# Two-layer hybrid trunk on one core: TensorE in program order for the experts of layer 1, PSUM banks and weight slots re-dealt, and two of four row tiles normalised on TensorE

## The chip, the cores and the metric

The kernel runs on one core of one Trainium2 chip, as one launch. The metric is the device time of that launch in microseconds. Before the change three runs took 1233.72, 1237.96 and 1239.21 us; the median, 1237.96 us, is the time before.

A core has TensorE (PE in the profile; PEld is its weight load), VectorE (DVE), ScalarE (ACT), GpSimd (POOL) and SyncE (SP). SP computes nothing here: its queue issues most of the transfers, in the order in which they stand in it. ACT and POOL issue some transfers too.

## The reference, cut to what matters

A stream of 256 latent rows and 256 context rows, 1024 wide, goes through two layers. Each layer has a mixer (recurrences and attention in layer 0, two chunked state models in layer 1) and then a mixture of experts. Only the second half matters for the change:

```
h  = rms_norm(x, norm2_g) * (1 + m4) + m3          # m3 is the shift, a row of 1024 for the latents
hc = rms_norm(xc, norm2_g) * (1 + mc4) + mc3       # context rows, layer 0 only
out = 0
for e in range(16):                                # two of the 16 experts per row, by a gate
    hid = silu(t @ w1[e]) * (t @ w3[e])
    out = out + gate[:, e:e+1] * (hid @ w2[e])
x = x + m5 * out
```

Layer 0 sends 512 rows through its experts, layer 1 only the 256 latent rows. The weights of 16 experts are 96 MB in each layer, and each is used once.

## The kernel before, in words

**Memory.** One big SBUF tile, `arena_f`, is cut by a small allocator (`Arena`): `F.get` hands out columns, `F.free` takes them back, and the next owner waits on the chip for the last reader of the columns. What is left over becomes weight slots of 2048 columns (1 MB each). The class `Stream` keeps the list of all weight pieces in the order of their use, and issues the next piece on SP's queue whenever a slot is free (L159). `ws.add(F.fits(2048) - FA[l])` in `finish` (L1294) turns all whole free blocks but FA into slots; L1341 does the same with FB, and L1447 in `moe` with RES; `experts_rows` and `experts_sum` add what is left (L1612 and L1671). For layer 1, `swap` (L1355) also turns the split buffers `arena_rw` and `arena_rr` into six slots once the mixer is done with them. By the allocator's own count L1294 finds ten free blocks in layer 1 and makes eight of them slots, and the stage of the experts ends up with 19.

**Order.** The program is traced from Python, and a planner then orders the instructions of each engine by its own model of costs and due times. So an engine need not follow the order of the source. Each engine runs its list in that order, and waits at the head of the list. The planner also keeps two engines off one PSUM bank: a matmul into one half of a bank waits while another engine reads the other half.

**Layer 0, from the router to the first expert (`moe`, L1364).** `finish` leaves in `H` the rows x * (1 + m4) * norm2_g, unnormalised, two tiles of 128 latent rows (t = 0, 1) and two of context rows (t = 2, 3), and has laid down in DRAM, in `hd`, the shift row broadcast to all 512 rows (four transfers of 512 KB on ACT's queue, L1292). When the row norms `rs` are known, L1386 scales each tile on ACT (128x1024), and L1387 has POOL add it to `hd` by an accumulating transfer, 512 KB each. Meanwhile DVE computes the routing. The first expert's rows are gathered from `hd` by an indirect transfer of POOL (`gather`, L1474), transposed by TensorE (L1521, `take`) and multiplied (`first`, `hidden`, `second` in `experts_rows`), with every fp32 weight split in two by ACT (L322) and DVE or POOL (L325) and three matmuls for each product (L331 to L333).

**Layer 1, experts (`experts_sum`, L1656).** Weights are used unsplit. For each pair of experts `take` (L1700) selects up to 64 rows for each by 32 matmuls with a one-hot matrix. `first(e)` multiplies with w1 and then w3, 32 matmuls each (L1714), two weight pieces each, into the two halves of one PSUM bank; after w1 ACT takes a tanh (L1720) and DVE forms u (L1721), after w3 DVE finishes u (L1723). `hidden` transposes u (L1729) and ACT copies it out (L1730). `second` multiplies with w2, 16 matmuls (L1741) with two pieces; DVE applies the gate (L1746) and POOL adds the rows to the output by an indirect transfer (`scatter`, L1479). `rows` (L1681, L1683) are four small matmuls per expert that give row numbers and gates. The source interleaves them: w1(e), hidden(e-1), every other time take, rows(e+1), w3(e), second(e-1). The stream of pieces has the same order: w1 and w3 of e+1 before w2 of e.

PSUM has eight banks; `bank` deals them by tag, four to "a" (used by `first`, `second`), three to "b", one to "m".

**The shift row.** `mod_half` (L402) computes the modulation rows in eight steps of two layers by three groups by two halves; the rows of a half end in `ms`, biased by a DVE add (L425), and ACT's queue writes them to the DRAM tile `md` (L442). For l = 0, g = 1 the partitions 64 up hold m3.

## Time and profile before

| | |
|---|---|
| median of three runs | 1237.96 us |
| the profiled execution: its own time / its span | 1241.31 us / 1239.5 us |
| mean granted TensorE clock | 0.952 |
| busy: PE / DVE / ACT / POOL | 88% / 63% / 42% / 29% of the span |
| moved by transfers | 318.83 MB, 257 GB/s over the span |

The span runs from the first to the last instruction. All times in the rows are microseconds from the start of the span; durations of single groups are in ns where it says so. Busy shares are averages over stages with different limits, so the stages are read one by one: router of layer 0 at about 336 to 366 us, experts of layer 0 to about 670, mixer of layer 1 to about 990, experts of layer 1 from 1003 to the end. "PEclk" 1.00 is the clock of 2.4 GHz, 0.50 that of 1.2 GHz. A row of the timeline may stand for several instructions of one line (xN), from the start of the first to the end of the last; the ends of matmuls are modelled and overlap the next start, so pace is read from start to start.

### The profile page before, as it was taken

How to read it: one execution, taken by the hardware profiler on the slowest of the kernel's cores; microseconds unless marked ns; L12 is line 12 of the kernel's file. 1: busy time of each engine (PE TensorE's matmuls, PEld its weight loads, DVE VectorE, ACT ScalarE, POOL GpSimd, SP SyncE). 2: the span in 40 equal slices, each digit the busy share in tenths (PEclk: the TensorE clock that was granted, in tenths of full speed). 3: DMA queues.
4: the chain of work that ended last, by engine and by line, in shares of the span. 5: the costliest groups of instructions: out<-in, count | busy, mean ns of one | idle time of the engine just before them, and what ended most of it. 6: DMA issues, size and time to landing. Idle time of an engine off the chain costs nothing. (4 is left out here: it accounts for less than half of the span.)

```text
span 1239.5 us, 17204 instructions
## 1 busy us (share of the span) xinstructions
PE 1088.7 (88%) x6462; PEld 775.7 (63%) x6462; DVE 776.1 (63%) x1363; ACT 520.4 (42%) x799; POOL 360.9 (29%) x229
## 2 busy tenths in 40 slices
PE   3998979999829999999999788988997779999986
PEld 1666655656717777777777456655776766665552
DVE  2566737664639999999988754898477553222111
ACT  3355624443517787877887332333343210000000
POOL 1331513333213544545430321244242301111111
PEclk9998989999959999999999788999999889999998
DMA  9663468457277999999993135332387599999993
GB/s 354 215 221 123 167 178 279 157 192 282 109 214 259 347 356 352 366 352 357 352 356 119 73 140 139 132 139 90 122 301 267 226 374 409 413 421 419 409 412 96
DMA packets 76826, 318.83 MB, mean 257 GB/s; under 512 B 21290, under 2 KB 27530, under 8 KB 47936
## 3 DMA queue, kind: packets, MB, share of 16 engines
q1 hardware_dynamic: 54368, 293.58, 62.1%
q0 software_dynamic: 7200, 12.30, 4.7%
q10 hardware_dynamic: 15168, 11.76, 3.5%
q8 instruction: 54, 0.88, 0.3%
q14 instruction: 36, 0.29, 0.1%
HBM read 310.48 MB, written 18.96 MB: 266 GB/s over the span
## 5 line engine op out<-in xcount | busy, mean ns | idle before, releaser
L322 ACT CAST arena_rw<-arena_f 128x1024 fp32r<-128x1024 f32 x256 | 264.8, 1049 | 179.1 <-PE b L333 112.0
L325 DVE TENSOR_TENSOR arena_rw<-arena_f,arena_rw 128x1024 fp32r<-128x1024 f32 x198 | 259.3, 1348 | 84.9 <-ACT arena_rw L322 84.7
L331 PE MATMUL b<-arena_rw,arena_rr 128*128 128x512 f32 (+1 forms) x736 | 276.5, 376 | 3.0 <-ACT arena_rr L1217 1.1
L332 PE MATMUL b<-arena_rw,arena_rr 128*128 128x512 f32 (+1 forms) x736 | 274.1, 373 | 0.0
L333 PE MATMUL b<-arena_rw,arena_rr 128*128 128x512 f32 (+1 forms) x736 | 272.7, 372 | 0.0
L325 POOL TENSOR_TENSOR arena_rw<-arena_f,arena_rw 128x1024 fp32r<-128x1024 f32 x58 | 143.7, 2478 | 239.6 <-ACT arena_rw L322 220.8
L331 PEld LDWEIGHTS b<-arena_rw,arena_rr 128*128 128x128 f32 x736 | 140.4, 191 | 39.3 <-issue 9.8
L333 PEld LDWEIGHTS b<-arena_rw,arena_rr 128*128 128x128 f32 x736 | 139.8, 191 | 27.5 <-issue 4.1
L332 PEld LDWEIGHTS b<-arena_rw,arena_rr 128*128 128x128 f32 x736 | 140.6, 191 | 23.8 <-issue 1.3
L1479 POOL DMA_INDIRECT out<-arena_f x16 | 24.9, 1557 | 220.7 <-DVE arena_f L1746 216.8
L420 PE MATMUL b<-arena_f,cs 128*32 128x256 f32 x768 | 68.5, 412 | 22.3 <-DMA arena_f<-in_modw 22.1
L331 PE MATMUL b<-arena_rr,arena_rw 128*128 128x512 f32 (+1 forms) x192 | 75.3, 396 | 3.1 <-ACT arena_rw L322 1.4
L1714 PE MATMUL b<-arena_f 128*64 128x256 f32 x608 | 72.2, 381 | 4.5 <-DVE arena_f L1721 4.5
L333 PE MATMUL b<-arena_rr,arena_rw 128*128 128x512 f32 (+1 forms) x192 | 72.6, 381 | 3.9 <-DVE arena_rw L325 3.9
L1720 ACT ACTIVATE arena_f<-b 128x256 f32<-128x256 f32 x16 | 6.1, 384 | 165.9 <-PE b L1714 165.9
L332 PE MATMUL b<-arena_rr,arena_rw 128*128 128x512 f32 (+1 forms) x192 | 73.7, 385 | 0.8 <-POOL arena_rr L510 0.8
L1714 PEld LDWEIGHTS b<-arena_f 128*64 128x64 f32 x608 | 47.2, 137 | 26.8 <-DVE arena_f L1721 6.4
L420 PEld LDWEIGHTS b<-arena_f,cs 128*32 128x32 f32 x768 | 20.7, 112 | 55.3 <-issue 27.0
L1714 PE MATMUL b<-arena_f,arena_f 128*64 128x256 f32 x416 | 49.9, 381 | 1.9 <-DVE arena_f L1721 1.9
L331 PEld LDWEIGHTS b<-arena_rr,arena_rw 128*128 128x128 f32 x192 | 37.4, 196 | 18.7 <-issue 7.4
L1479 POOL DMA_INDIRECT yd<-arena_f x14 | 32.0, 2284 | 52.0 <-ACT arena_f L1569 52.0
L1474 POOL DMA_INDIRECT arena_f<-hd,arena_f x16 | 27.3, 1706 | 64.1 <-DVE arena_f L1514 50.5
(372 smaller groups left out, 1673.9 us busy)
## 6 DMA issues: line engine op xcount, KB each, us to landing
arena_f<-in_moe SPq DMA_DIRECT2D x192, 1024.0 KB
arena_f<-in_modw SPq DMA_DIRECT2D x96, 512.0 KB
arena_f<-in_wod SPq DMA_DIRECT2D x18, 1024.0 KB
arena_f<-in_wev SPq DMA_DIRECT2D x14, 1024.0 KB
arena_f<-md ACTq DMA_DIRECT2D x8, 512.0 KB
arena_f<-in_tok SPq DMA_DIRECT2D x4, 512.0 KB
yd<-arena_f SPq DMA_DIRECT2D x4, 512.0 KB
hd<-md ACTq DMA_DIRECT2D x4, 512.0 KB
```

The source lines that it names most:

```text
L322: nc.scalar.copy(h, raw)
L325: eng.tensor_tensor(l, raw, h.bitcast(F32), op=OP.subtract)
L331: nc.tensor.matmul(ps, ah, bh, start=first, stop=False)
L332: nc.tensor.matmul(ps, ah, bl, start=False, stop=False)
L333: nc.tensor.matmul(ps, al, bh, start=False, stop=last)
L420: nc.tensor.matmul(acc[32 * i:32 * i + 32, 0:256], self.cs[:, k, :], raw[:, i * 256:(i + 1) * 256], start=(k == 0), stop=(k == KC - 1))
L1474: self.nc.gpsimd.indirect_dma_start(out=xg, out_offset=None, in_=hd[:, :], in_offset=bass.IndirectOffsetOnAxis(ap=tk, axis=0), bounds_chec ...
L1479: self.nc.gpsimd.indirect_dma_start(out=yd[:, :], out_offset=bass.IndirectOffsetOnAxis(ap=dst, axis=0), in_=y, in_offset=None, bounds_chec ...
L1714: nc.tensor.matmul(p[64 * c:64 * c + 64, 256 * w:256 * w + 256], x[:, 4 * b + k], raw[:, 512 * k + 256 * c:512 * k + 256 * c + 256], start ...
L1720: nc.scalar.activation(u, p[:, 0:256], AF.Tanh, scale=0.5)
```

## The change

In layer 1, all TensorE instructions of the experts' loop are chained, each to the one traced before it, so that the planner must keep the order of the source (`in_order`). `first` takes one PSUM bank for w1 and another for w3. FA falls from 2 to 1 for both layers and RES from 3 to 2 for layer 0, so that one more block becomes a weight slot at those points.

In layer 0, the tiles of the latent rows no longer go through accumulating transfers. `mod_half` splits m3 into three bf16 terms (five small DVE operations and two more transfers on ACT's queue for each half) and stores them in `mb2`; `finish` loads them to three partitions, `S3`, and lays down the shift in DRAM for the context rows only. In `moe` ACT builds two diagonal matrices of `rs`; for each latent tile and each half of 512 columns TensorE multiplies the diagonal with `H` and adds ones times `S3` in the same bank, ACT copies the sum back over `H`, and SP's queue stores the tile to `hd` as a plain transfer. The context tiles are scaled and accumulated as before.

```diff
@@ -13,6 +13,8 @@
 AX = mybir.AxisListType
+PE = mybir.EngineType.PE
+NOSYNC = mybir.DependencyInfo(mybir.DependencyClass.NoSync, mybir.DependencyReason.DATA)
 
 P = 128
 D = 1024
@@ -235,8 +237,8 @@
 BQ = "sync"
 HR = 4
 HP = 0, 1, 0, 0
-RES = 3, 3
-FA = 2, 2
+RES = 2, 3
+FA = 1, 1
 FB = 9, 9
 NYY = 4
 WMK = 3
@@ -269,6 +271,22 @@
     def bank(self, tag="b"):
         self.n += 1
         return self.ps.tile([P, 512], F32, tag=tag, name=f"b{self.n}", bufs={"a": 4, "b": 3, "m": 1}[tag])
+
+    @contextmanager
+    def in_order(self, engine):
+
+        cur = self.nc.cur_bb
+        traced = cur.bb.instructions
+        last = traced[-1]
+        yield
+        traced = cur.bb.instructions
+        start = next(k for k in reversed(range(len(traced))) if traced[k] is last or traced[k].name == last.name) + 1
+        prev = None
+        for i in traced[start:]:
+            if i.engine == engine:
+                if prev is not None:
+                    self.tc.add_manual_dep(i, prev.name, NOSYNC, reason="in_order")
+                prev = i
 
     def dbg(self, name, ap):
         if self.dbgf is not None:
@@ -441,6 +459,16 @@
             for i in range(4):
                 nc.scalar.dma_start(self.md[l, g][:, h, i // 2, 256 * (i % 2):256 * (i % 2) + 256],
                                     ms[32 * i:32 * i + 2])
+            if (l, g) == (0, 1):
+
+                pt = F.get(3, 256, dt=BF)
+                for i in range(3):
+                    nc.vector.tensor_copy(pt[64:, i], ms[64:])
+                    if i < 2:
+                        nc.vector.tensor_tensor(ms[64:], ms[64:], pt[64:, i], op=OP.subtract)
+                for q in range(2):
+                    nc.scalar.dma_start(self.mb2[:, :, h, 256 * q:256 * q + 256], pt[64 + 32 * q:66 + 32 * q])
+                F.free(pt)
             F.free(ms)
         else:
             self.mr[l, h] = ms
@@ -1283,14 +1311,14 @@
 
         H = [F.get(2, D) for s in range(ns)]
         if ns == 2:
-
             self.hd = self.dp.tile([4 * P, D], F32, name=f"hd{l}")
-            for s in range(2):
-                src = self.md[l, 1][s, :, 1].rearrange("(o h) c -> o h c", o=1)
-                for i in range(2):
-                    t = 2 * s + i
-                    nc.scalar.dma_start(self.hd[t * P:(t + 1) * P, :].rearrange("p (h c) -> p h c", h=2),
-                                        src.to_broadcast([P, 2, 512]))
+
+            self.S3 = F.get(D, dt=BF)
+            nc.scalar.dma_start(self.S3[0:3], self.mb2[0].rearrange("i h c -> i (h c)"))
+            src = self.md[l, 1][1, :, 1].rearrange("(o h) c -> o h c", o=1)
+            for t in range(2, 4):
+                nc.scalar.dma_start(self.hd[t * P:(t + 1) * P, :].rearrange("p (h c) -> p h c", h=2),
+                                    src.to_broadcast([P, 2, 512]))
         self.ws.add(F.fits(2048) - FA[l])
 
         lg, hfR = [self.bank("m"), self.bank("a")][0:ns], Ring(F, 2, 2, 256)
@@ -1380,12 +1408,21 @@
             stt(L[:, t], lp[:, 32 * t:32 * t + 32], rs[:, t:t + 1], self.bR[:, t // 2], op0=OP.mult, op1=OP.add)
         if ns == 2:
 
-            H, hd = hd, self.hd
-            for t in range(nt):
-                h = H[t // 2][:, t % 2]
-                nc.scalar.activation(h, h, AF.Copy, scale=rs[:, t:t + 1])
-                nc.gpsimd.dma_start(hd[t * P:(t + 1) * P, :], h, accum_op=OP.add)
-            F.free(*H)
+
+            H, hd, dgR = hd, self.hd, F.get(2, P)
+            for t in range(2):
+                nc.scalar.activation(dgR[:, t], self.ident, AF.Copy, scale=rs[:, t:t + 1])
+            for t in range(2):
+                h, g = H[0][:, t], H[1][:, t]
+                nc.scalar.activation(g, g, AF.Copy, scale=rs[:, 2 + t:3 + t])
+                nc.gpsimd.dma_start(hd[(2 + t) * P:(3 + t) * P, :], g, accum_op=OP.add)
+                for c in range(2):
+                    sl, ps = slice(512 * c, 512 * c + 512), self.bank("a")
+                    nc.tensor.matmul(ps, dgR[:, t], h[:, sl], start=True, stop=False)
+                    nc.tensor.matmul(ps, self.oneb[0:3], self.S3[0:3, sl], start=False, stop=True)
+                    nc.scalar.copy(h[:, sl], ps)
+                nc.sync.dma_start(hd[t * P:(t + 1) * P, :], h)
+            F.free(*H, self.S3, dgR)
         tmp = []
 
         def T(n):
@@ -1705,22 +1742,24 @@
 
         def first(e):
             x = xs.pop(e)
-            p = self.bank("a")
+            ps = []
             for w in range(2):
+                p = self.bank("a")
                 for b in range(2):
                     raw = self.ws.take()
                     for k in range(4):
                         for c in range(2):
-                            nc.tensor.matmul(p[64 * c:64 * c + 64, 256 * w:256 * w + 256], x[:, 4 * b + k],
+                            nc.tensor.matmul(p[64 * c:64 * c + 64, 0:256], x[:, 4 * b + k],
                                              raw[:, 512 * k + 256 * c:512 * k + 256 * c + 256],
                                              start=(b == 0 and k == 0), stop=(b == 1 and k == 3))
                     self.ws.done(raw)
+                ps.append(p[:, 0:256])
                 if w == 0:
                     u = uR()
-                    nc.scalar.activation(u, p[:, 0:256], AF.Tanh, scale=0.5)
-                    nc.vector.scalar_tensor_tensor(u, u, 1.0, p[:, 0:256], op0=OP.add, op1=OP.mult)
+                    nc.scalar.activation(u, ps[0], AF.Tanh, scale=0.5)
+                    nc.vector.scalar_tensor_tensor(u, u, 1.0, ps[0], op0=OP.add, op1=OP.mult)
                 yield
-            nc.vector.scalar_tensor_tensor(u, u, 0.5, p[:, 256:512], op0=OP.mult, op1=OP.mult)
+            nc.vector.scalar_tensor_tensor(u, u, 0.5, ps[1], op0=OP.mult, op1=OP.mult)
             us[e] = u
 
         def hidden(e):
@@ -1746,20 +1785,21 @@
             nc.vector.scalar_tensor_tensor(y, py, gt, G2, op0=OP.mult, op1=OP.mult)
             self.scatter(half, y, dst)
 
...
+        with self.in_order(PE):
+            take(0)
+            rows(0)
+            for e in range(NE + 1):
+                f = first(e) if e < NE else iter(())
+                next(f, None)
+                if e:
+                    hidden(e - 1)
+                if e % 2 and e < NE - 1:
+                    take(e // 2 + 1)
+                if e + 1 < NE:
+                    rows(e + 1)
+                run_all(f)
+                if e:
+                    second(e - 1)
         F.free(ohR, phR, gtR, ddR, xR, uR, utR, yR, G2)
 
         def xt(xT, ohb, oh, cols):
@@ -1873,6 +1913,7 @@
         nc, tc, I, F, R = self.nc, self.tc, self.I, self.F, self.R
         w, m = self.sources(stages)
         self.ws, self.wm = Stream(nc, F, w, 2048), Stream(nc, F, m, 1024)
+        self.mb2 = self.dp.tile([2, 3, 2, 512], BF, name="mb2")
         self.md = {(l, g): self.dp.tile([2, 2, 2, 512], F32, name=f"md{l}{g}") for l in range(2) for g in (1, 2)}
         self.mr, self.sh, self.a2 = {}, [F.get(2, KC) for l in range(2)], [F.get(2, KC) for l in range(2)]
         self.rest = self.mods((1, 1), (1, 2)) if "l1" in stages else iter(())
```

## Rows read from the trace of the kernel before

**Rows 1.** Stretches: stretch, length, busy PE, PEld, DVE, ACT, POOL; PEclk, DMA share, GB/s.
```profile
500.00:525.00 25.00, 24.25 (x122) 19.48 (x121) 22.80 (x23) 20.16 (x25) 13.85 (x6) 1.00 1.00 369
...
985.00:990.00 5.00, 2.92 (x13) 2.11 (x14) 1.98 (x3) 1.92 (x5) 1.31 (x2) 0.52 0.01 2
...
1150.00:1200.00 50.00, 45.62 (x338) 25.61 (x336) 9.09 (x22) 2.27 (x6) 4.66 (x3) 1.00 1.02 413
```

**Rows 2.** Timeline of layer 0's router: start, length, engine, line [idle before it].
```profile
339.32 4.26 ACT L1386 ACTIVATE arena_f<-arena_f 128x1024 f32<-128x1024 f32 x4 [1.00 <-DVE arena_f L298]
...
340.79 2.90 POOL L1387 DMA_DIRECT2D hd<-arena_f  x3 [14.91 <-ACT arena_f L1386]
...
357.87 1.11 POOL L1474 DMA_INDIRECT arena_f<-hd,arena_f  x1 [13.13 <-DMA hd<-arena_f]
...
366.57 1.94 PE L1521 MATMUL b<-mskt,arena_f 128*128 128x128 f32 x8 [18.14 <-DMA arena_f<-hd,arena_f]
```

**Rows 3.** The stretch of the four accumulating transfers, columns as in rows 1.
```profile
342.00:356.00 14.00, 1.26 (x30) 1.03 (x30) 7.26 (x36) 1.82 (x4) 2.53 (x3) 0.50 0.88 152
```

**Rows 4.** Waits of SP's queue at 930 to 1000, 1003 to 1075, 1075 to 1200: total, times, longest.
```profile
SPq L159 <- PE b L333: 15.1, 1, 15.1
...
SPq L159 <- PE b L1714: 40.7, 17, 6.6
...
SPq L159 <- DMA arena_f<-in_moe: 104.7, 48, 3.5
```

**Rows 5.** Timeline of TensorE: the start of layer 1's experts.
```profile
1002.96 6.80 PE L1700 MATMUL b<-arena_f 128*128 128x128 f32 x32 [1.33 <-DVE arena_f L1452]
...
1009.77 1.95 PE L1714 MATMUL b<-arena_f,arena_f 128*64 128x256 f32 x16
```

**Rows 6.** Timeline of TensorE, 1020 to 1032 us: one of each step.
```profile
1020.93 0.44 PE L1729 MATMUL b<-mskt,arena_f 128*128 128x128 f32 x2
1021.20 3.74 PE L1700 MATMUL b<-arena_f 128*128 128x128 f32 x32
...
1024.95 3.67 PE L1714 MATMUL b<-arena_f 128*64 128x256 f32 x32
1028.45 3.60 PE L1741 MATMUL b<-arena_f 128*64 128x512 f32 x16
1031.89 0.39 PE L1714 MATMUL b<-arena_f 128*64 128x256 f32 x2
```

**Rows 7.** Timeline of TensorE: two experts in the second half of the stage.
```profile
1139.90 3.62 PE L1714 MATMUL b<-arena_f 128*64 128x256 f32 x32
1144.46 3.67 PE L1714 MATMUL b<-arena_f 128*64 128x256 f32 x32 [0.94 <-DVE arena_f L1721]
...
1169.89 3.62 PE L1714 MATMUL b<-arena_f,arena_f 128*64 128x256 f32 x32
```

**Rows 8.** Waits of TensorE, 1003 to 1230 us: total us, times, longest.
```profile
PE b L1714 <- DVE arena_f L1721: 6.3, 7, 0.9
PE b L1729 <- DVE arena_f L1723: 3.7, 7, 0.5
```

**Rows 9.** Stretches at the end of the weight stream, columns as in rows 1.
```profile
1218.00:1219.00 1.00, 1.00 (x12) 0.70 (x10) 0.00 (x0) 0.00 (x0) 0.00 (x0) 1.00 0.19 41
1219.00:1220.00 1.00, 1.00 (x14) 0.65 (x10) 0.00 (x0) 0.00 (x0) 0.00 (x0) 1.00 0.00 0
```

**Rows 10.** Timeline of all engines, 1221 us to the end.
```profile
1225.33 0.75 DVE L1746 SCALAR_TENSOR_TENSOR arena_f<-b,arena_f 128x512 f32<-128x512 f32 x1 [4.12 <-PE b L1741]
...
1226.36 1.55 POOL L1479 DMA_INDIRECT out<-arena_f  x1 [11.06 <-DVE arena_f L1746]
...
1228.77 0.75 DVE L1746 SCALAR_TENSOR_TENSOR arena_f<-b,arena_f 128x512 f32<-128x512 f32 x1 [2.68 <-PE b L1741]
1231.80 1.55 POOL L1479 DMA_INDIRECT out<-arena_f  x1 [3.88 <-DMA out<-arena_f]
```

**Rows 11.** Operations on L425, all times: duration in ns, minimum/median/maximum.
```profile
L425 DVE TENSOR_TENSOR arena_f<-b,arena_f x12: 405/424/425, 27.1 to 957.7; 128x256 f32<-128x256 f32 x12
```

More of the change, by code (lines that the diff above doesn't have):

```diff
@@ L1 @@
-from contextlib import ExitStack
+from contextlib import ExitStack, contextmanager
 import numpy as np
@@ L1747, in second @@
             self.scatter(half, y, dst)
-        take(0)
-        rows(0)
-        for e in range(NE + 1):
-            f = first(e) if e < NE else iter(())
-            next(f, None)
-            if e:
-                hidden(e - 1)
-            if e % 2 and e < NE - 1:
-                take(e // 2 + 1)
-            if e + 1 < NE:
-                rows(e + 1)
-            run_all(f)
-            if e:
-                second(e - 1)
+        with self.in_order(PE):
[13 more added lines that the diff above has]
+                    second(e - 1)
         F.free(ohR, phR, gtR, ddR, xR, uR, utR, yR, G2)
```

## The prediction

> **What bounds the kernel now.** I read the page's forty slices first, then a table of stretches, and then each stage that the change touches in its own timeline and waits. The experts of layer 0 are bound by the compute engines: in a stretch of 25 us TensorE is busy for 24.25 and VectorE for 22.8, and the weights are there in time [rows 1]. So what an earlier start saves there is kept, and a slot more in the middle of that stage is worth nothing. In front of it lies a hole: ScalarE scales four tiles in 4.26 us, GpSimd issues four accumulating transfers from 340.79 on, then waits 13.13 us for them, and gathers the first expert's rows at 357.87; TensorE sits idle 18.14 us until 366.57 [rows 2]. The routing is not what ends this wait; the transfers are.
>
> Layer 1's experts have two limits side by side. The transfers run full: DMA share 1.02 at 413 GB/s [rows 1]. Early on SP's queue waits for TensorE to release slots (40.7 us in 1003 to 1075), later only for its own earlier transfers (104.7 us in 1075 to 1200) [rows 4]. TensorE for its part never stands waiting for a weight: its waits are for DVE [rows 8]. Both hold because TensorE lags behind the stream: the last weights land by about 1218.9, when the share falls to zero [rows 9], but the last gate operation starts at 1228.77 [rows 10], though one half of `second`, under 2 us, is all that needs the last piece. What ends last there is TensorE.
>
> **Layer 1, TensorE's order and the banks.** From start to start, one step costs [rows 6]: hidden 0.27, take with rows 3.75, a w half 3.50, second 3.44. Two experts in the order of the source take four halves (14.0), two seconds (6.9), two hiddens (0.5), one take and two rows (3.9): 25.3 us, 12.7 for one. In the second half the planner put w1, w3 and hidden of one expert in a row. Then w3's matmuls wait 0.94 us for DVE's reading of the same bank, and hidden waits for DVE's last operation; two experts take 1169.89 - 1139.90 = 30.0 us [rows 7]. Over the stage these two waits are 6.3 and 3.7 us [rows 8]. Bound to the source, `second` of the expert before (3.44 us) lies between w3 and hidden, which covers the second wait; a bank of its own for w3 removes the first. Four "a" banks for three uses per expert give each bank back one expert after its reader is done, so I cost that at nothing; the cover is w1 of the next expert, and without it the price is the 0.9 of rows 8.
>
> From w1 of expert 0 at 1009.77 [rows 5] the whole list needs 32 halves (112.0), 16 seconds (55.0), 7 takes with rows (26.3), 16 hiddens and the other rows (6): 199 us, so TensorE could be done at 1209. It is then the weights that end last. The new chain makes the queue wait at its head for each piece, but the pieces come in the same order, so nothing is held that could run.
>
> **Layer 1, the slot.** The stream stands idle before the stage: DMA share 0.01 in 985 to 990 [rows 1], because SP's head waits 15.1 us for the mixer's last matmuls to release the six late slots [rows 4]. The new slot stands ahead of these in the list, and its columns held keys of the state model, freed before the merge; so 1 MB more lands in this hole. At 413 GB/s that is 2.5 us off the rest of the stream. Bounds: 0, if the columns come free only with the late slots, and 2.5. I take 2.5: the wait in front is for an engine, not for transfers.
>
> So the last piece lands at 1216.4. `second(14)` ends on the piece two before it, 1211.4 + 1.75 (half of 3.44) = 1213.2. Now the gate operation of 14 at 1225.33 led to the last scatter at 1231.80, 6.47 us later, since that waits for the scatter before it [rows 10]; so the last scatter starts at 1219.7 (second(15) is done at 1218.1, and its own path would give 1219.2). Against 1231.80 that is **12.1 us**. Without the slot it is 9.6.
>
> **Layer 0, the transfers.** The four accumulating transfers fill 14 us at a share of 0.88 [rows 3], 12.3 us of all engines, 3.1 for each of 512 KB. Two remain: 6.2. The two plain stores move 1 MB, at 413 GB/s 2.5 us. If all share the engines, 8.7 us replace 12.3, a gain of 3.6; if the stores fit into the gaps, 6.2. ScalarE's list: two 128x128 copies (at most half a 128x256 operation of the kind in rows 11, so 0.2 each) go ahead of the first scaling, then two scalings of 1.07, then four copies of 512 columns, bounded by half a scaling, 0.53, below and a whole one above: 4.7 to 6.8 us against 4.26 [rows 2]. TensorE, otherwise idle, adds four fp32 matmuls of 512 columns and four in bf16; `second` does eight pairs of such fp32 ones in 3.44 [rows 6], 0.43 a pair, so 0.43 each and 0.86 at half the clock, the bf16 ones no more: 7 us at most, partly beside ScalarE. The stores are then issued by about 347, on an SP queue whose earlier weights have gone; behind them wait the pieces for slots cut from `H`, which must wait for the same transfers anyway, and GpSimd's gather, which waits for all four. GpSimd issues two accumulations less (2.90 for three, about 1 us each), but it only waits afterwards: nothing. Rows 3 show engines that are nearly full, so I stay near the lower end and take **4 us**.
> The Trainium skill says in "DMA: Bandwidth & Descriptors", section "Issuing engines are not separate DMA queues", that transfers issued by different engines run on the same 16 DMA engines and interleave. By it the lower end, 3.6, would be the gain; the share of 0.88 agrees.
>
> **The other edits.** The splitting of m3 adds ten DVE operations no larger than the bias add of 0.42 [rows 11]: 4.2 us of an engine that is busy 63% of the span, behind the mixer's matmuls. I take 0; 4.2 if that cover is gone. Two broadcasts less into `hd` take 1 MB off ACT's queue around 190; ACT's extra small transfers there offset it: 0, between -2.5 and +2.5 by the same rate. FA and RES for layer 0: 0, since that stage is bound by compute [rows 1]. `S3` waits on ACT's queue for its columns; what stands behind it is weight casts, and the cover is split weights already waiting: 0, and up to a few us if ACT arrives early.
>
> **Sum.** 12.1 + 4 = 16.1 us. The profiled execution took 1241.3 us, 1.8 more than its span; that gives 1225.2. It lay 3.35 us over the median, so against the median I forecast **1222**. A measurement of this kernel can tell about 0.5%, 6.2 us, from no change.
>
> **Rivals.**
> TensorE stays the bound: other waits take the place of those removed, and the weights stay ahead of it. For it: some ten us of waits are all that rows 8 show as removable, and take must wait for DVE in its new place. Against: DVE is busy 9 of 50 us [rows 1]. Then 6.3 (the bank) + 4 = 10.3, so 1228. 12%.
> The stores land as late as the accumulates did, because SP's or ACT's list puts them late: only layer 1 gains, 1226. 11%.
> The clock: a TensorE that catches up with the weights idles between pieces. The profile shows 32 matmuls in 6.63 us after a pause, against 3.57 at full clock [rows 5, 6]: 3 us for one such fall. Against it: waits of 0.9 in every expert left PEclk at 1.00 [rows 1, 7]. One fall at the end and one more: 1226. 5%.
> The Trainium skill, "TensorE: Matmul & The Clock Gate", section "HAM oscillation", has a kernel in which waits for transfers let the array fall back each time; it speaks against feeding TensorE to the limit. By that rule these 3 us would come back at each wait.
> The change doesn't do what it says, the planner's order having been as good or the slot not there in time: layer 0's 4 us alone, 1234. 8%.
> Slower: bound to the source, TensorE's head waits at `rows`, take and hidden for DVE or ACT each time, and nothing behind can pass. At 1.3 us, the wait once seen at the first take [rows 5], six such waits in two experts are 3.9 for one: 16.6, and TensorE ends 62 us after 1209, at 1271 and not by 1230: 1238 + 41 - 4, about 1275. It decides from 1.9 us per expert, where 1209 becomes 1239 and outweighs layer 0's 4 us by more than can be told from no change. 4%.
>
> **How the numbers follow.** Forecast 60% (1216 to 1227: the slot's 0 to 2.5, the transfers' 0.5 to 6.2, the small edits). The rivals hold 40%, of which those at 1226 to 1228 are taken in; the range 1214 to 1231 leaves out the last two, 12%, and some luck on the good side. Faster by over 0.5% (below 1231.8) are all but these two: 0.88; same 0.08; slower 0.04.
>
> **What would show it.** Right: TensorE's rows in layer 1 repeat w1, hidden, take, rows, w3, second to the end; the wait of L1714 for L1721 is gone and in the last experts TensorE waits for weights; the stream of weights ends 2.5 us earlier than layer 0 alone would shift it; the gather of expert 0 comes 3 to 6 us sooner. Wrong: TensorE still waits for DVE at L1700 or L1729; PEclk falls after 1150; the first gather waits for a transfer of SP's queue; the share in the hole before the experts is unchanged.

## The result, and the profile after

The changed kernel takes **1222.08 us** (median of four runs, 1220.29 to 1228.52); the kernel before, timed beside it, 1238.59 us. The ratio is 0.9869, 95% interval 0.9826 to 0.9912: faster by more than the 0.5% that the prediction can tell from no change, and on the forecast of 1222. A second round of six runs gave 1226.41 us and 0.9891 (0.9854 to 0.9927). The profiled execution took 1223.47 us with a span of 1221.3, 18.2 us less than the 1239.5 of before.

The sum is right, but not each of its terms. Five marks divide both profiles: the first operation of the router's rs chain on VectorE (L487 before, L515 after), the first and the last start of the matmuls that gather an expert's rows in layer 0 (L1521, L1558), the first `take` of layer 1 (L1700, L1737), and the end. So the stretch called mixer and router begins with the last work of layer 0's experts, some 30 us.

| stretch (us) | before | after | difference | forecast |
|---|---|---|---|---|
| to layer 0's rs chain | 336.7 | 342.1 | +5.4 | 0 |
| rs chain to the first expert's matmul | 29.8 | 22.8 | -7.0 | -4 |
| layer 0's experts | 275.1 | 275.5 | +0.4 | 0 |
| layer 1's mixer and router | 361.3 | 354.9 | -6.4 | 0 |
| layer 1's experts to the end | 236.6 | 226.0 | -10.6 | -12.1 |
| span | 1239.5 | 1221.3 | -18.2 | -16.1 |

**Layer 0's router.** The timeline of the changed kernel, lines that answer to [rows 2], each from start and length in us:

```profile
342.09 0.16 DVE L515 TENSOR_TENSOR arena_f<-arena_f 128x4 f32<-128x4 f32 x1 [0.81 <-ACT arena_f L1349]
...
345.18 1.13 PE L1421 MATMUL b<-arena_f 128*128 128x512 f32 x2 [0.83 <-ACT arena_f L1414]
346.24 0.38 PE L1422 MATMUL b<-arena_f,bfs 3*128 3x512 bf16 x1
...
346.78 1.07 POOL L1418 DMA_DIRECT2D hd<-arena_f  x1 [6.17 <-DVE arena_f L1442]
348.61 0.91 POOL L1418 DMA_DIRECT2D hd<-arena_f  x1 [0.75 <-ACT arena_f L1417]
348.80 2.92 SPq L1424 DMA_DIRECT2D hd<-arena_f  x2
358.62 1.11 POOL L1511 DMA_INDIRECT arena_f<-hd,arena_f  x1 [9.10 <-DMA hd<-arena_f]
363.36 0.94 ACTq L500 DMA_DIRECT2D arena_f<-md  x2
364.91 1.94 PE L1558 MATMUL b<-mskt,arena_f 128*128 128x128 f32 x8 [10.55 <-DMA arena_f<-hd,arena_f]
```

Everything starts 5.4 us later, so the gather at 358.62 stands a little behind the 357.87 of [rows 2]. Counted from the rs chain it comes 4.6 us sooner (16.5 instead of 21.1): the four us of the forecast. The two profiles of layer 1's edits alone, whose layer 0 code is that of before, have 18.6 and 19.8 us there; against them the gain is 2.0 and 3.3. The stretch of the transfers has thinned out, as the row that answers to [rows 3] shows (stretch, length, busy PE, PEld, DVE, ACT, POOL; PEclk, DMA share, GB/s):

```profile
344.00:358.00 14.00, 7.07 (x46) 2.77 (x45) 10.27 (x53) 5.23 (x10) 1.98 (x2) 0.82 0.70 176
```

The share is 0.70 instead of 0.88. From the gather to the first matmul it takes 6.3 us instead of 8.7, which the forecast did not have. In the kernel before, two loads of `md` (512 KB each, L472, from 355.56 on) and three weight pieces (from 357.06 on) were issued within 2.5 us of its gather; here one weight piece goes out at 357.87, and the loads follow at 363.36. That this is the cause was not tried.

**Layer 1's experts.** TensorE's timeline at the place of [rows 7]:

```profile
1136.67 3.62 PE L1752 MATMUL b<-arena_f 128*64 128x256 f32 x32
1140.23 0.44 PE L1768 MATMUL b<-mskt,arena_f 128*128 128x128 f32 x2
1140.50 3.74 PE L1737 MATMUL b<-arena_f 128*128 128x128 f32 x32
...
1144.25 3.67 PE L1752 MATMUL b<-arena_f 128*64 128x256 f32 x32
1147.75 3.60 PE L1780 MATMUL b<-arena_f 128*64 128x512 f32 x16
1151.19 3.62 PE L1752 MATMUL b<-arena_f 128*64 128x256 f32 x32
...
1162.13 1.90 PE L1752 MATMUL b<-arena_f,arena_f 128*64 128x256 f32 x16
```

The order is w1, hidden, take, (rows), w3, second, and nothing waits in it: two experts take 1162.13 - 1136.67 = 25.5 us, by the forecast's list 25.3, where [rows 7] have 30.0. In the table of TensorE's waits from 1000 us on (waiting line, what it waited for, total us, times, longest) VectorE is gone:

```profile
PE b L1752 <- DMA arena_f<-in_moe: 4.2, 7, 1.1
PE b L1780 <- DMA arena_f<-in_moe: 1.7, 3, 0.6
```

[Rows 8] had 6.3 and 3.7 us of waits for VectorE; here TensorE waits for weights. SP's longest wait for the mixer's last matmuls ahead of the stage, 15.1 us in [rows 4], is shorter too:

```profile
SPq L161 <- PE b L351: 9.9, 1, 9.9
```

Four rows of the timeline's end show who ends last now, beside [rows 10]:

```profile
1200.69 1.95 PE L1752 MATMUL b<-arena_f 128*64 128x256 f32 x16 [1.00 <-DMA arena_f<-in_moe]
...
1210.61 1.94 PE L1780 MATMUL b<-arena_f,arena_f 128*64 128x512 f32 x8 [0.20 <-SPq L1842]
1212.60 0.75 DVE L1785 SCALAR_TENSOR_TENSOR arena_f<-b,arena_f 128x512 f32<-128x512 f32 x1 [4.21 <-PE b L1780]
1213.94 1.55 POOL L1516 DMA_INDIRECT out<-arena_f  x1 [3.72 <-DVEq L1842]
```

The last piece of weights lands at 1210.6, half a `second` follows at once, and TensorE is done 2.0 us after it; before, it was done 9.9 us after (1228.7 against 1218.8). That distance, from the last landing to TensorE's end, says in one number which of the two is the bound, and the experiments below are read by it.

### The profile page after: what moved, and what is told of

Same layout as the page of the kernel before. It is cut to its first block, busy times and chain, and to the rows that moved or that the text cites. A ratio compares the mean times of both kernels' runs of the same rounds, so it can differ in the third digit from the quotient of the medians.

```text
span 1221.3 us, 17265 instructions
## 1 busy us (share of the span) xinstructions
PE 1090.1 (89%) x6474; PEld 769.0 (63%) x6474; DVE 780.0 (64%) x1373; ACT 521.0 (43%) x803; POOL 357.8 (29%) x227
## 5 line engine op out<-in xcount | busy, mean ns | idle before, releaser
L438 PE MATMUL b<-arena_f,cs 128*32 128x256 f32 x768 | 69.1, 417 | 16.8 <-DMA arena_f<-in_modw 16.6
L1752 PE MATMUL b<-arena_f 128*64 128x256 f32 x672 | 77.9, 381 | 4.1 <-DMA arena_f<-in_moe 4.0
L349 PEld LDWEIGHTS b<-arena_rr,arena_rw 128*128 128x128 f32 x192 | 37.3, 195 | 20.0 <-issue 6.1
L584 POOL TENSOR_TENSOR arena_f<-arena_f 128x512 f32<-128x512 f32 x21 | 29.6, 1414 | 62.4 <-DVE arena_f L581 57.9
L351 PEld LDWEIGHTS b<-arena_rr,arena_rw 128*128 128x128 f32 x192 | 37.5, 195 | 12.7 <-DVE arena_rw L343 4.1
```

Source lines behind the costliest of these rows:

```text
L349: nc.tensor.matmul(ps, ah, bh, start=first, stop=False)
L351: nc.tensor.matmul(ps, al, bh, start=False, stop=last)
L438: nc.tensor.matmul(acc[32 * i:32 * i + 32, 0:256], self.cs[:, k, :], raw[:, i * 256:(i + 1) * 256], start=(k == 0), stop=(k == KC - 1))
L584: (nc.vector if last and c == 3 else nc.gpsimd).tensor_tensor(xs, xs, tmp, op=OP.add)
L1752: nc.tensor.matmul(p[64 * c:64 * c + 64, 0:256], x[:, 4 * b + k], raw[:, 512 * k + 256 * c:512 * k + 256 * c + 256], start=(b == 0 and k = ...
```

## The experiments

All but the ratio are us; the last column is TensorE's end after the last landing of weights. Stages are those of the table above; layer 0's experts took 274.6 to 275.9 us in all kernels but the one with one bank (279.1, with TensorE's clock lower).

| kernel | time (runs) | ratio to before | to rs chain | rs to first matmul | layer 1 mixer, router | layer 1 experts | TensorE after weights |
|---|---|---|---|---|---|---|---|
| before | 1238.59 (4) | 1 | 336.7 | 29.8 | 361.3 | 236.6 | 9.9 |
| changed | 1222.08 (4) | 0.9869 | 342.1 | 22.8 | 354.9 | 226.0 | 2.0 |
| changed, again | 1226.41 (6) | 0.9891 | 341.8 | 22.5 | 355.2 | 226.3 | 2.0 |
| layer 1's edits alone | 1230.93 (12) | 0.9954 | 335.7 | 27.2 | 357.2 | 224.1 | 2.0 |
| the same, again | 1227.72 (10) | 0.9900 | 337.1 | 29.4 | 355.8 | 224.5 | 2.0 |
| layer 0's edits alone | 1236.66 (12) | 0.9979 | 341.1 | 22.8 | 354.5 | 238.0 | 11.7 |
| no order | 1223.26 (4) | 0.9877 | 341.3 | 22.8 | 355.0 | 226.3 | 2.0 |
| one bank | 1226.32 (4) | 0.9897 | 342.6 | 23.2 | 354.6 | 225.5 | 2.0 |
| slot alone in layer 1 | 1237.89 (10) | 0.9990 | 341.5 | 22.9 | 354.8 | 238.3 | 13.2 |
| no slot in layer 1 | 1225.78 (4) | 0.9858 | 342.3 | 22.9 | 354.8 | 229.1 | 2.0 |
| split on GpSimd | 1220.84 (4) | 0.9823 | 338.7 | 22.4 | 355.0 | 226.4 | 2.0 |
| shift in fp32 | 1226.31 (4) | 0.9869 | 339.4 | 28.6 | 356.7 | 224.6 | 2.0 |
| layer 0's old slots | 1218.79 (4) | 0.9824 | 342.5 | 23.9 | 350.4 | 227.3 | 2.0 |
| old slots, split on GpSimd | 1217.71 (6) | 0.9819 | 339.1 | 22.7 | 346.9 | 229.1 | 2.0 |

The intervals of the ratios are about 0.003 wide on either side for the kernels with ten or more runs and 0.004 to 0.006 for the others. One warning on the quoted expectations: where they give 333 to 334 us as the start of the rs chain without layer 0's edits, the wrong row was read. It starts at 335.7 to 337.1 in the three profiles without those edits, so the loss ahead of the router is 5 us and not 8. Some stage lengths in them rest on the same misreading; the table has the right ones.

**Layer 1's edits alone.** Layer 0's code as before, without the split of m3, with `RES = 3, 3` and `FA = 2, 1`:

```
-            self.S3 = F.get(D, dt=BF)
...
+            for s in range(2):
+                src = self.md[l, 1][s, :, 1].rearrange("(o h) c -> o h c", o=1)
...
+                nc.gpsimd.dma_start(hd[t * P:(t + 1) * P, :], h, accum_op=OP.add)
```

> Layer 1's edits alone (TensorE order, bank per half, slot); layer 0 as before. Read from the two profiles, the changed kernel's 18.2 us (span 1239.5 to 1221.3) lie so: layer 0 up to its experts only 1.3 us (5.4 lost ahead of the router, 6.6 gained in it), 6.3 in layer 1's mixer and router, which no edit touches, and 10.6 in layer 1's experts. Theory 1: the 6.3 come with layer 1's edits (the slot ahead of the mixer's list shifts its schedule); then the span is 1239.5 - 16.9 = 1222.6, ratio to before about 0.986. Theory 2: the 6.3 come with layer 0's edits (other timing, other schedule); then 1239.5 - 10.6 = 1229, ratio 0.991. The forecast had 12.1 us for this part: 0.990. By each theory layer 0's experts start where they did before, at 366.6.

Measured: 1230.93 us, ratio 0.9954 (0.9925 to 0.9983). The profile took 1218.8 us and was the shortest of twelve executions, which reach to 1238.28. In it layer 1's experts take 224.1 us with TensorE 2.0 us behind the weights. The stretch of the mixer took 357.2 us, 4.1 less than before, so neither theory has all of it. What the profile says of the stages holds; that this kernel's median lies so far above its profile it does not explain.

**Layer 0's edits alone.** Layer 1's code as before: no order, one bank, `FA = 1, 2`, `RES = 2, 3`.

```
-        with self.in_order(PE):
+        if True:
...
-FA = 1, 1
+FA = 1, 2
```

> Layer 0's edits alone (normalisation on TensorE, plain stores, its slots); layer 1 as before: no binding of TensorE's order, one bank, no slot more. Theory 1: layer 0's experts start 1.3 us sooner and nothing else moves: span 1238, ratio 0.999. Theory 2: the mixer of layer 1 gains its 6.3 us here; TensorE is the bound in layer 1's experts as before, so its end moves with its start: 1239.5 - 7.6 = 1232, ratio 0.994. The forecast had 4 us: 0.997. By both, the router's rs chain is 5.4 us later than in the kernel before (342.1 against 336.7).

Measured: 1236.66 us, ratio 0.9979 (0.9956 to 1.0002), span 1232.2. Theory 2's span: layer 0 gives little by itself (its experts start at 363.9), the mixer is 6.8 us shorter here as well, and TensorE, still 11.7 us behind the weights, is the bound to the end. The interval of the ratio includes no change, though: the runs give this kernel 0 to 5 us, where the two profiles differ by 7.3. The mixer's gain shows with either half of the change; the section on the prediction says where it lies.

**Order and bank, one at a time.** Without the order:

```
-        with self.in_order(PE):
+        if True:
```

> The changed kernel without the binding of TensorE to the order of the source; a bank per half and the slot stay. Theory 1: the bank takes away the 6.3 us of waits of w3's matmuls for DVE, the 3.7 us of hidden's waits for DVE stay because the planner still puts hidden right behind w3; TensorE then ends about 4 us after the weights let it: span 1221.3 + 4 = 1225, ratio to before 0.989. Theory 2: the bank is all that matters, the order nothing: 1221.3. Rival: without the bond the planner puts the steps as before and TensorE stays 10 us behind the stream: 1231.

With the order and one bank:

```
-                p = self.bank("a")
...
-                            nc.tensor.matmul(p[64 * c:64 * c + 64, 0:256], x[:, 4 * b + k],
+                            nc.tensor.matmul(p[64 * c:64 * c + 64, 256 * w:256 * w + 256], x[:, 4 * b + k],
```

> The changed kernel with one bank for both halves of an expert again; the binding to the order stays. Theory 1: bound to the source, hidden and rows lie between w1 and w3, so DVE has read w1's half before w3 starts and the bank is worth little: under 1 us more than the changed kernel's span of 1221.3, and the wait of w3's matmuls for DVE stays under 1 us in sum. Theory 2: the bank is what counts: w3 waits 0.9 us in each of 16 experts, 15 us of TensorE, of which some 10 were slack to the weights: 1226 or more.

Measured: 1223.26 and 1226.32 us; layer 1's experts take 226.3 and 225.5 us, as with both. So each of the two is enough, and they do not add. The waits of TensorE without the order, from 1000 us on:

```profile
PE b L1768 <- DVE arena_f L1762: 4.2, 8, 0.5
PE b L1780 <- SPq L1842: 1.6, 3, 0.6
```

Hidden's wait for VectorE is still there, as expected, but the bank has taken away w3's, and 4.2 us is less than the room that is left below the weights. With one bank:

```profile
PE b L1751 <- DVE arena_f L1759: 6.6, 9, 1.1
PE b L1737 <- DVE arena_f L1489: 1.3, 1, 1.3
```

Theory 1 of the one bank expected under 1 us of waits of w3 for VectorE. There are 6.6, though hidden and rows lie in between; in the half of the experts without `take` that cover is too short. It costs nothing all the same: TensorE still ends 2.0 us after the weights.

**The slot, with and without the rest.** The slot alone (no order, and one bank by the diff above):

```
-        with self.in_order(PE):
+        if True:
...
+                            nc.tensor.matmul(p[64 * c:64 * c + 64, 256 * w:256 * w + 256], x[:, 4 * b + k],
```

> The changed kernel with layer 1's slot alone: no binding of TensorE's order, one bank for both halves. From layer 1's first rows to the end the kernel without all three (layer 0's edits alone) took 238.0 us, the changed kernel 226.0, order without bank 225.5, bank without order 226.3. Theory 1: TensorE is the bound without order and bank, so the slot gives nothing: 237 to 238 here, span about 1233. Rival: the slot does the work and order and bank give little: 226 to 228 here, span about 1223.

No slot (order and bank stay):

```
-FA = 1, 1
+FA = 1, 2
```

> The changed kernel without layer 1's extra slot. Theory 1: weights end last, so the slot's megabyte comes back at the end: from layer 1's first rows to the end 226.0 + 2.5 = 228.5 us, last weight landing 2.5 us later against the first rows, span about 1224. Rival: the slot is what moved the end: 236 to 238, span 1233. Second rival: it gave nothing, 226.

Measured: 1237.89 us and 1225.78 us. With the slot alone the stage takes 238.3 us, with neither slot nor the others 238.0: nothing, as the first theory has it. The waits of its TensorE are like those of before [rows 8]:

```profile
PE b L1751 <- DVE arena_f L1759: 7.5, 8, 0.9
PE b L1767 <- DVE arena_f L1761: 4.2, 8, 0.5
```

Once order or bank has taken TensorE out of the way, the slot is worth 229.1 - 226.0 = 3.1 us. From the first `take` the last landing comes after 217.9 us without it and 215.2 with it, 2.7 us; the forecast had 2.5. The wait of SP for the mixer's last matmuls, ahead of the stage, is 8.7 us with the slot alone and 16.6 with layer 0's edits alone, 9.9 in the changed kernel and 17.0 without the slot: it does its work in the hole, as forecast.

**The split of m3.** The ten operations on GpSimd:

```
-                    nc.vector.tensor_copy(pt[64:, i], ms[64:])
+                    nc.gpsimd.tensor_copy(pt[64:, i], ms[64:])
...
+                        nc.gpsimd.tensor_tensor(ms[64:], ms[64:], pt[64:, i], op=OP.subtract)
```

> The changed kernel with the ten operations that split m3 into three bf16 rows on GpSimd instead of VectorE. With them on VectorE the router's rs chain starts at 341 to 343 us in four profiles, without the layer 0 edits at 333 to 334. Theory 1: VectorE's part is the cause (8.5 us of operations, up to 2.5 us each): then rs starts at 335 or so and the experts of layer 0 start 6 us sooner, span about 1215, ratio 0.982. Theory 2: it is what the split does to the planner's order around 200 to 225 us, wherever it runs, or GpSimd's queue takes VectorE's place: rs stays at 340 to 343, span as the changed kernel's.

No split at all; the shift row is loaded from `md` and added in fp32:

```
...
-                    nc.tensor.matmul(ps, self.oneb[0:3], self.S3[0:3, sl], start=False, stop=True)
+                    nc.tensor.matmul(ps, self.msk("ones")[0:1], self.S3[0:1, sl], start=False, stop=True)
```

> The changed kernel without the split: the shift row is loaded once in fp32 and added by an fp32 matmul with one row of ones in place of the bf16 one with three. Theory 1: the split and its order are the cause of the 8 us lost ahead of the router: rs at 333 to 335, and four fp32 matmuls in place of four bf16 ones cost at most 4 x 0.75 = 3 us in the router, partly hidden beside ScalarE's copies: experts of layer 0 from 357 to 359 instead of 364.9, span about 1214, ratio 0.980 to 0.984. Theory 2: the loss comes from the broadcasts and slots, not the split: rs at 341 to 343, span 1221 to 1224.

Measured: 1220.84 us with the rs chain at 338.7, and 1226.31 us with it at 339.4. Both theories hold in part: with the split off VectorE the chain starts some 3 us sooner, but not at 336.7. In the changed kernel's timeline the price of the split is plain:

```profile
141.16 2.19 POOL L684 TENSOR_TENSOR arena_f<-arena_f 128x512 f32<-128x512 f32 x1 [6.33 <-DVE arena_f L682]
142.23 1.40 DVE L468 TENSOR_TENSOR arena_f<-arena_f 64x256 f32<-64x256 f32 x1
...
192.83 2.87 POOL L343 TENSOR_TENSOR arena_rw<-arena_f,arena_rw 128x1024 fp32r<-128x1024 f32 x1 [0.50 <-ACT arena_rw L340]
193.58 2.40 DVE L468 TENSOR_TENSOR arena_f<-arena_f 64x256 f32<-64x256 f32 x1
...
196.34 0.42 DVE L468 TENSOR_TENSOR arena_f<-arena_f 64x256 f32<-64x256 f32 x1
```

The same subtraction takes 0.42 us by itself and 2.40 where a GpSimd operation with two SBUF inputs is running: that one ends at 195.70, the subtraction at 195.98. Its four executions range from 0.42 to 2.53 us, and the three long ones each end 0.28 us after such an operation of GpSimd. By the Trainium skill, "SBUF — State Buffer", section "Who interferes with whom", a VectorE instruction with two SBUF inputs contends with a GpSimd instruction that reads SBUF, and the port pair that the two share is an exclusive lock; the trace agrees.

The other 2 to 3 us are lost between 203 and 224 us, in the state model's heads. TensorE's timeline there:

```profile
209.88 1.13 PE L783 MATMUL b<-arena_f 64*128 64x256 f32 x4 [2.05 <-ACT arena_f L775]
210.94 0.63 PE L438 MATMUL b<-arena_f,cs 128*32 128x256 f32 x6
213.38 3.78 PE L770 MATMUL b<-arena_f 64*128 64x512 f32 x4 [1.81 <-DVE arena_f L755]
216.96 1.91 PE L783 MATMUL b<-arena_f 64*128 64x256 f32 x4
```

In the kernel before, modulation matmuls (L420) fill these two gaps:

```profile
210.68 2.77 PE L420 MATMUL b<-arena_f,cs 128*32 128x256 f32 x20
213.38 2.15 PE L742 MATMUL b<-arena_f 64*128 64x512 f32 x4
215.37 1.02 PE L755 MATMUL b<-arena_f 64*128 64x256 f32 x4
```

L742 (L770 above) takes 2.15 us and L755 (L783) 1.02. In the changed kernel those matmuls stand elsewhere in the list, and the granted clock over 203 to 224 is 0.76, where it was 0.91 over 202 to 220.5. The gap of 1.81 us is there in all eleven profiles with layer 0's edits, with the split on VectorE, on GpSimd or nowhere, so the split is not its cause. Which of layer 0's edits is, stays open.

The fp32 shift loses in the router what it saves ahead of it. Its clock is 0.58 from the rs chain to the first matmul, and each fp32 matmul (two records) takes 2.07 us, with ScalarE's copies behind them:

```profile
347.18 2.07 PE L1413 MATMUL b<-arena_f,mskt 1*128 1x512 f32 x2
349.18 2.08 PE L1412 MATMUL b<-arena_f 128*128 128x512 f32 x2
353.30 0.59 ACT L1414 COPY arena_f<-b 128x512 f32<-128x512 f32 x1 [3.32 <-PE b L1413]
```

The second store is issued only at 357.92. The bf16 form with three rows costs 0.38 at the full clock and is well worth its split.

**Layer 0's slots.** The old numbers with all else changed, and the same with the split on GpSimd:

```
-RES = 2, 3
-FA = 1, 1
+RES = 3, 3
+FA = 2, 1
```

> The changed kernel with layer 0's slot numbers of before (RES 3, FA 2 for layer 0); all else as changed. In every profile with layer 0's edits, with or without the split, TensorE's list between 200 and 225 us stands in another order than before and loses some 3 us there (waits of 2.05 us for ScalarE and 1.81 us for VectorE, and a window at half the clock). Theory 1: the slot numbers cause that order: rs starts at 338 to 339 instead of 342.1, span about 1218. Theory 2: the order comes from the other edits: rs at 341 to 343, span 1220 to 1223. By both, layer 0's experts take 275 to 276 us as before; were the slot worth something there, more.

> The split on GpSimd and layer 0's slot numbers of before together. Theory 1 (slots cause the order, VectorE's split the rest): rs at 334 to 335, layer 0's experts start at 357 to 358, span about 1214, time 1216, ratio 0.981. Theory 2 (slots do nothing): as with the split on GpSimd alone, rs 338.7, experts from 361.1, span 1218, time 1220 to 1221, ratio 0.985.

Measured: 1218.79 and 1217.71 us, the two shortest medians here; by the ratios (0.9824 and 0.9819) they cannot be told from the split on GpSimd alone (0.9823). The rs chain stays at 342.5 and 339.1, so the slots are not the cause of TensorE's order either: the first theory fell. The gain lies where neither theory looked, in layer 1's mixer and router: 350.4 and 346.9 us, where all kernels with the new slot numbers have 354.5 to 356.7. The waits of the changed kernel between 960 and 990 us begin with

```profile
DVE arena_f L1329 <- DMA arena_f<-md: 7.1, 1, 7.1
```

and its timeline has the load on ACT's queue and the operation that waits for it:

```profile
963.13 0.39 ACTq L500 DMA_DIRECT2D arena_f<-md  x1
...
974.89 0.69 DVE L1329 TENSOR_TENSOR arena_f<-arena_f 128x512 f32<-128x512 f32 x1 [7.08 <-DMA arena_f<-md]
```

This is the row that scales layer 1's latent rows, 512 KB after its broadcast. It is in use 11.8 us after its issue, beside weights at a DMA share of 0.96 (960 to 980 us). With layer 0's old slots it goes out ten us sooner and nobody waits for it:

```profile
953.58 0.39 ACTq L500 DMA_DIRECT2D arena_f<-md  x1
...
971.93 0.69 DVE L1329 TENSOR_TENSOR arena_f<-arena_f 128x512 f32<-128x512 f32 x1 [1.46 <-POOL arena_f L584]
```

The kernel before had the same wait, 5.2 us after an issue at 972.48. The old numbers do this only beside layer 0's edits: layer 1's edits alone have them too, with layer 0's code of before, and there the load goes out at 961.83 and 966.62 and is waited for, 7.5 and 5.8 us. Part of the gain is given back: layer 1's experts take 227.3 and 229.1 us. The weights end last there too (2.0 us before TensorE), and a stage that starts sooner has had less of the stream ahead of it.

**Twice the same.** Layer 1's edits alone and the changed kernel, each run again without an edit:

> Layer 1's edits alone once more: its first profiled execution had a span of 1218.8 us, but the median of its runs was 1230.9. Theory 1: what differs between its executions lies ahead of layer 1's experts, in the four accumulating transfers and in how long TensorE's clock stays low: this profile's span is nearer 1229, layer 1's experts again take 224 to 226 us, and the stages before take some 8 us more than in the first one. Theory 2: layer 1's experts vary: TensorE waits for weights, its clock falls, and they take 230 us or more in a slow execution.

> The changed kernel once more, with a second profile, to tell what of the first profile's account is the program and what one execution. If the account holds: rs at 341 to 343 us, the router up to the first expert's matmuls 22 to 24 us, layer 0's experts 275 to 276, layer 1's mixer and router 354 to 356 with a wait of VectorE for the scale row's load of 5 to 7 us, layer 1's experts 226 to 227, span 1220 to 1225, ratio to before 0.985 to 0.989. Rival: the wait for the scale row and the place of TensorE's low clock are chance, and the mixer and router take 350 or 360 us this time. Were the kernel with layer 0's old slots and the split on GpSimd (1217.7, all of its runs under 1219.1) no better than this one, this one's runs would reach below 1219 as often.

Layer 1's edits alone gave 1227.72 us over ten runs (1223.33 to 1235.21) and a profile of 1222.2 us, short again, so it cannot show what lengthens the other executions; this stays open. Its stages ahead of layer 1's experts took 3 us more than the first time, the experts 224.5. The changed kernel's account held to 0.4 us in every stage, with the same wait of 7.1 us for the scale row: it is the program and not one execution. Its ten executions in all lie between 1220.29 and 1228.91; the six of the kernel with old slots and the split on GpSimd between 1215.08 and 1219.09. The better version is therefore probably **old slots and GpSimd's split**, some 4 to 9 us under the changed kernel by the medians. The two were timed on different chips, with the kernel before at 1238.6 to 1241.4 beside them, and the intervals of their ratios still overlap (0.9773 to 0.9865 against 0.9826 to 0.9912 and 0.9854 to 0.9927).

## Why the prediction was right, and where not

**TensorE's order and the banks: right, with one correction.** That TensorE and not the weights ended last, and that its waits for VectorE made it so, is shown: without both edits it ends 11.7 and 13.2 us after the weights, with either 2.0. Order and bank without the slot make the stage 238.0 - 229.1 = 8.9 us shorter; the forecast had 9.6 without the slot. The correction: the text let one edit take away one wait and the other the second, and the rival with the bank alone was priced at 6.3 us. The runs show that either is enough, because the slack between TensorE's work and the weights is wider than the wait that is left. Of the step "one take and two rows" the size held to 0.2 us in 25.3.

**The slot: right**, 2.7 us of landing and 3.1 of time against 2.5, and so is the condition on it: with TensorE as the bound it is worth nothing. The sign that was named for it, a stream that ends 2.5 us earlier than layer 0 alone would shift it, is not there: the last landing is at 1210.6, with layer 0's edits alone at 1210.1 (215.2 and 215.9 us after the first `take`). Order and bank without the slot have 217.9; why the stream ends later with them was not traced.

**The end: right in its mechanism.** The last landing came at 1210.6; the forecast's 1216.4 less layer 0's 4 us is 1212.4. The stage began 7.6 us sooner than before, 3.6 more than forecast, but it gave 10.6 us and not 12.1: the landing follows the first `take` by 215.2 us, where the forecast's 2.5 would have made 213.4 of the 215.9 before. From landing to the last scatter it took 3.3 us, as in the forecast (1216.4 to 1219.7); the scatter before had landed at 1213.2 and the gate operation ended at 1213.35, so its two paths lie within 0.2 us of each other.

**Layer 0's transfers: right at the gather, short behind it.** Forecast 4 us; 4.6 by the two profiles, 2.0 to 4.6 by all three with the old code. The stores were issued 9.3 us after the rs chain's start by the second of them, where the text put them ten after it. What was missed are the 2.4 us from the gather to the first matmul. One step had the wrong size without harm: an fp32 matmul of 512 columns (two records in the trace) was put at 0.43 us from those of `second`, whose rows have weights of 128*64 [rows 6]; with 128*128 it takes 1.13.

**"The other edits": this step failed.** "I take 0; 4.2 if that cover is gone" was wrong in the value taken: split and TensorE's new order together cost 5.4 us ahead of the router, of which 2.7 to 3.4 go with the split. The 0.42 us that priced it was right only for an operation that runs beside an idle GpSimd. "FA and RES for layer 0: 0" was right for layer 0's experts and wrong in sum: with the rest of the change, the numbers shift the load of a row in layer 1 by ten us, and the old ones are 3 us better by the medians of 1222.08 and 1218.79, a difference within the intervals of the two ratios; the spans of the profiles differ by 2.0.

**What was not forecast at all** is the 6.4 us in layer 1's mixer and router. They are there with layer 0's edits alone (6.8) and for the most part with layer 1's alone (4.1 and 5.5). Most of it is one wait of the kernel before. Two rows of its waits over 940 to 1000 us, and VectorE's timeline there:

```profile
POOL arena_f L1275 <- DMA arena_f<-in_rout: 8.7, 1, 8.7
DVE arena_f L1277 <- POOL arena_f L1275: 6.8, 1, 6.8
```

```profile
943.83 0.18 DVE L1159 RECIPROCAL arena_f<-arena_f 128x4 f32<-128x4 f32 x1
950.83 0.61 DVE L1277 TENSOR_REDUCE arena_f<-arena_f 128x32 f32<-128x256 f32 x1 [6.82 <-POOL arena_f L1275]
951.36 0.68 DVE L1164 TENSOR_TENSOR arena_f<-arena_f 128x512 f32<-128x512 f32 x1
```

A reduction for the router (L1277) stands in VectorE's list ahead of the mixer's own operations, and waits 6.8 us for GpSimd, which waits for the router's weights (`in_rout`, issued on ACT's queue at 941.54). In the changed kernel the same reduction (L1305) stands at 949.20, behind the operations that it held up, and waits for nothing. L1164 (L1192 there) comes at 941.09, 10.3 us sooner; at 940 us the lead is 4.0. Of the 10.3, 2.8 are given back by 990 us, 1.9 of them to the scale row (a wait of 7.1 us against 5.2). With layer 1's edits alone the reduction waits 1.5 and 1.2 us, in the eleven profiles with layer 0's edits not at all. So it is the planner's order, which either half of the change moves, that gained here. The 2.7 us by which the lead grows from 641 to 940 us were not traced, and as only one profile of the kernel before exists, how long that load takes in its other executions stays open.

That the total came out to 0.1 us is in part luck: the 6.4 us that were not forecast and 3.0 more than forecast in the router stand against 5.4 lost ahead of it and 1.5 that layer 1's experts lack, and the six later runs have a median 4.3 us higher.

**The rivals.** That TensorE stays the bound or waits at its head is excluded by the waits; the only wait at `take` is the 1.3 us at the first. The clock did not fall in layer 1's experts, in spite of ten waits for weights of up to 1.1 us: PEclk is 1.00 from 1150 us to TensorE's end at 1212.5. The case in "TensorE: Matmul & The Clock Gate", section "HAM oscillation", of the Trainium skill in which the array falls back at every wait for a transfer, is not met here: the clock stayed at its upper level through each of these waits. The sign named for a wrong step in layer 0, that the gather waits for SP's transfer, came true by 1.6 us: the second plain store lands at 357.7, the second accumulation at 356.1.

## What to carry to other kernels

When two resources run side by side, measure how long the slower one goes on after the last transfer; edits that shorten it are worth no more than that distance together, and a buffer slot is worth nothing until it is used up. Before costing an added VectorE operation at its own length, look at what GpSimd runs beside it: with two SBUF inputs it can take six times as long. After a change of slot counts look again at the small loads of rows: their place in a queue can move, and a late one can cost more than the slot gives. When a stage that no edit touches gets faster, look for the wait that went away before crediting chance: in a list that an engine runs in order, one operation placed ahead of its input holds up all behind it.

## What the runs showed of the hardware that was not expected

The subtraction of 64x256 that waits for GpSimd: 0.42 us alone, 1.40, 2.40 and 2.53 beside it. A 512 KB load on ACT's queue took 9.9 and 11.8 us to its use beside pieces of 1 MB, at a DMA share of 0.90 and 1.00 over those stretches. In the router TensorE was busy for 7.07 us of 344 to 358 at a granted clock of 0.82, before for 1.26 us at 0.50 in the like stretch [rows 3]. Being busy is not enough for the upper level, though: with the shift in fp32 the clock fell while TensorE ran its pairs of fp32 matmuls, one with 128 rows and one with a single row, without a pause, and from 345.2 to 357.2 us it was busy for 12.00 of 12 us at 0.50. Why is open.

One observation has no explanation here: kernels with four accumulating transfers vary more from execution to execution (layer 1's edits alone 1220.67 to 1238.28; before 1228.39 to 1249.47 over all its runs beside the experiments) than those with two (layer 0's edits alone 1234.28 to 1241.83 in twelve runs, the slot alone 1235.26 to 1239.79 and the changed kernel 1220.29 to 1228.91 in ten each). That the transfers cause it was not tried.
